# Conditional expert code: arms left out for the lower ranks, and the whole-array arm moved behind the others in one lane

## The chip, the cores and the metric

The kernel runs on one core of one Trainium2 chip, in one launch. The metric is device time in microseconds. Before the change the median of 3 runs is 1930.11 us (1925.82 to 1934.0). All rows below come from one profiled execution of 1932.14 us, whose span from the first to the last instruction is 1930.4 us.

The engines are TensorE (PE: matmuls and transposes; PEld is its weight loads), VectorE (DVE), ScalarE (ACT), GpSimd (POOL) and SyncE (SP, which issues the DMAs). Each engine has a sequencer of its own that runs its part of the program; a "q" behind the name (PEq) means the sequencer, which executes branches, register loads and semaphore instructions.

## The reference

Two trunk layers run over 256 latent and 256 context tokens of width 1024. Layer 0 mixes tokens with a gated position MLP and has a dense SwiGLU; layer 1 mixes with a bidirectional gated recurrence, and its channel mixer is a mixture of eight SwiGLU experts, of which each token uses two. Only that mixture is touched here. In the reference every expert runs over all tokens, and the weight of an unchosen expert is zero:

```python
logits = (hf @ w_router).astype(jnp.float32)
top_val, top_idx = lax.top_k(logits, TOP_K)            # TOP_K = 2, 8 experts
probs = jax.nn.softmax(top_val, axis=-1)
combine = jnp.sum(jax.nn.one_hot(top_idx, N_EXPERTS) * probs[..., None], axis=1)
for e in range(N_EXPERTS):                             # 1024 -> 3584 -> 1024 each
    out = out + combine[:, e:e + 1] * swiglu(hf, w_gate[e], w_up[e], w_down[e])
```

So 512 token places are shared among eight experts, and no expert has more than 256. How many each one gets is known only at run time.

## The kernel before

From about 868 us on the kernel runs the mixture; what comes earlier is the same in both versions. After the router, DVE counts the tokens of each expert and sorts: rank 0 is always expert 0, ranks 1 to 7 are the other experts by falling count. A table `Q` (12 rows of 8 numbers: positions, weights, counts) is permuted into the order of the ranks by one large multiply with a permutation mask and one reduce (L1354, L1356), giving `Qr`, whose integer copy `cnti` the sequencers load into registers: `rv`, the rows of an expert that its base unit takes (up to 128), and `ro`, the rows that go over into a second, "over" unit (L1229, L1230). SP loads seven base addresses of weights from it as well (L1360). A count of 65 to 96 is split into 64 base rows and the rest as over rows; otherwise only what exceeds 128 goes over.

Weights stream from memory in pieces of 1 MB (L222). The 3584 hidden columns are cut into seven chunks of 512. A whole region (kind "R") is one chunk of one expert: six pieces, gate and up matmuls (both at L1250), the down matmuls (L1277) of the chunk one or two regions earlier, transposes of its hidden block ahead of these (L1268), ACT's silu and DVE's product (L1283). Kind "F" has only the down part; "O" and "G" gather the next expert's rows (L1207, L1212), "S" scatters results (L1289).

Two lanes of regions are merged into one list by a fixed rule (`moe_regions`). The full lane holds ranks 1, 2, 3, the other lane ranks 0, 7, 6, 5, 4. Their regions alternate in stretches: rank 7 runs beside rank 1, rank 6 beside rank 2, rank 5 beside the end of 2 and the start of 3, rank 4 beside rank 3. The list is unrolled: each region is code of its own on every engine.

Inside a region the code has arms, chosen by `region()`. The base unit has three: n = 1, the whole 128x128 array, for more than 64 rows (`If` at L1317); n = 2, tiles of 64 rows with two parts of the contraction side by side, for 33 to 64 (`If` at L1320); and n = 4, tiles of 32 rows, for 32 or fewer. Then, where `ro > 0` (L1324), the over unit has two: n = 1 for more than 32 rows (L1325), else n = 4. For n = 2 and n = 4 the parts are added up by ACT and DVE (L1256 to L1260). One DVE, one ACT and one PE sequencer take each branch for themselves. An arm that is not taken is code that is jumped over. An over gather (L1235) and an over scatter (L1417) stand behind `If ro > 0` too.

In the order of a program a row "MATMUL ... x8" is eight matmuls, each of which the trace shows as two PE rows and two PEld rows. The four transposes of L1268 are two instructions each. So an arm of a whole region, with 24 matmuls and 4 transposes, is 104 instructions of PE.

With this data the trace shows these arms: rank 1 takes n = 1 and over n = 4; rank 2 takes n = 1 without over; rank 3 takes n = 2 and over n = 4; ranks 4 and 5 take n = 2; ranks 0, 6 and 7 take n = 4. Ranks 0, 2 and 4 to 7 have no over rows.

Of the kernel before, what the change touches and what calls it, by code (L numbers as in the profile page):

```python
# [9 lines left out]
F32 = mybir.dt.float32  # L10
F32R = mybir.dt.float32r
BF16 = mybir.dt.bfloat16
I32 = mybir.dt.int32
AF = mybir.ActivationFunctionType
ALU = mybir.AluOpType
AX = mybir.AxisListType

P = 128
# [4 lines left out]
NE = 8  # L23
# [245 lines left out]
def block_kernel(ctx, tc, xin, pos, cst, rows, wsT, adaS, adaT, wA, lruG, wr, wM, out):  # L269
    nc = tc.nc  # L270
    ACT, DVE, PE = nc.scalar, nc.vector, nc.tensor
# [37 lines left out]
    v = [va[:, 0], va[:, 1], vb[:, 0], vb[:, 1]]  # L309
# [724 lines left out]
    mp = ctx.enter_context(pool("mp", 1, "right"))  # L1034
    R = ExitStack()
    rp = R.enter_context(pool("rp", 1, "right"))
# [112 lines left out]
    pb = bank()  # L1149
# [2 lines left out]
    PE.matmul(pb[:, 8:16], tri, sb[:, 1], start=False, stop=True)  # L1152
    PE.matmul(pb[:, 16:24], onb, sb[:, 0], start=True, stop=False)
    PE.matmul(pb[:, 16:24], onb, sb[:, 1], start=False, stop=True)
    Q = mp.tile([P, 12, NE], F32, name="Q")
    posm, comb, few, m64, cb_, co_, e42 = Q[:, 0:2], Q[:, 2:4], Q[:, 4:8], Q[:, 8], Q[:, 9], Q[:, 10], Q[:, 11]
    DVE.scalar_tensor_tensor(posm, pb[:, 0:16].rearrange("p (t e) -> p t e", t=2), 1.0, sb, op0=ALU.add, op1=ALU.mult)
    cf = pb[:, 16:24]
    DVE.tensor_scalar(m64, cf, 64.0, 64.0, op0=ALU.is_gt, op1=ALU.mult)
    DVE.scalar_tensor_tensor(m64, cf, 96.0, m64, op0=ALU.is_le, op1=ALU.mult)  # L1160
    DVE.tensor_scalar(co_, cf, -128.0, None, op0=ALU.add)
    DVE.tensor_add(co_, co_, m64)
    DVE.tensor_scalar(co_, co_, 0.0, None, op0=ALU.max)
    DVE.tensor_sub(cb_, cf, co_)
    for n, (v, lim, m) in enumerate(((cb_, 64, 64), (cb_, 32, 32), (co_, 32, 64), (co_, 32, 32))):
        DVE.tensor_scalar(few[:, n], v, float(lim), -float(m), op0=ALU.is_le, op1=ALU.mult)
    dup = mp.tile([P, 2, P], F32, name="dup")
    DVE.memset(dup, 0.0)
    DVE.memset(dup[:, 0, 64:128], 1.0)
# [17 lines left out]
    class Expert:  # L1187
        def __init__(self, r, tab):
            self.e, self.s, self.n = r, LAG[r] - 1, (1, 2, 3).index(r) if r in (1, 2, 3) else (0, 7, 6, 5, 4).index(r)
            self.posm, self.comb, self.few, self.m64 = tab[:, 0:2], tab[:, 2:4], tab[:, 4:8], tab[:, 8, r:r + 1]  # L1190
            self.hh = hs_[self.s]

    def weigh(E, G, GT, ps, b):
# [25 lines left out]
    def gather_parts(E):  # L1219
        G = m2.tile([P, 2, P], F32, tag=f"G{E.s}", bufs=1, name="G")  # L1220
        sl_ = m2.tile([P, P], F32, tag="sl", bufs=1, name="sl")
        x = m2.tile([P, 8, P], F32, tag=f"x{E.s}", bufs=1, name="x")
        GT = m2.tile([P, 256], F32, tag=f"GT{E.s}", name="GT")
        ps = m2.tile([P, 1], F32, tag=f"ps{E.s}", name="ps")
        E.base = Unit(x, None, tg[:, E.s], GT, ps)

        def last():
            weigh(E, G, GT, ps, nb[0]())
            E.rv = nc.values_load(cnti[0:1, 0, E.e:E.e + 1], engines=ENG, min_val=0, max_val=128)  # L1229
            E.ro = nc.values_load(cnti[0:1, 1, E.e:E.e + 1], engines=ENG, min_val=0, max_val=128)  # L1230
        return [lambda: onehot(E, G, sl_, 0), lambda: gather(x, G, 0, nb[0]()), lambda: gather(x, G, 4, nb[0]()), last]

    def gather_over(E):
        U = E.over
        with tc.If(E.ro > 0):  # L1235
            onehot(E, Gu, slu, 1)
            gather(U.x, Gu, 0, bks[2 * par[0]])
            gather(U.x, Gu, 4, bks[2 * par[0] + 1])
            weigh(E, Gu, U.GT, U.ps, bks[2 * par[0]])

# [44 lines left out]
    def scatter(GT, src):  # L1285
        for hf in range(2):
            for t in range(2):
                b = nb[0]()
                PE.matmul(b, GT[:, t * P:(t + 1) * P], src[:, hf * 512:(hf + 1) * 512], start=True, stop=True)  # L1289
                a = acc[:, t, hf * 512:(hf + 1) * 512]  # L1290
                DVE.tensor_add(a, a, b)  # L1291
# [21 lines left out]
    def region(E, c, raws):  # L1313
        p0, p1 = bks[2 * par[0]:2 * par[0] + 2]
        lag = LAG[E.e]
        a = (p1, p0, p1, E.base.y, raws, c == lag, c == NCH + lag - 1, *hsel(E, c, E.hh))
        with tc.If(E.rv > 64) as c1:  # L1317
            chunk(E.base, 1, *a)
        with c1.Else():
            with tc.If(E.rv > 32) as c2:  # L1320
                chunk(E.base, 2, *a)
            with c2.Else():
                chunk(E.base, 4, *a)
        with tc.If(E.ro > 0):  # L1324
            with tc.If(E.ro > 32) as c3:  # L1325
                over(E, c, 1, raws)
            with c3.Else():
                over(E, c, 4, raws)
# [3 lines left out]
    E = exps[0]  # L1332
# [11 lines left out]
    DVE.tensor_scalar(ke[:, 0, 0:1], ke[:, 0, 0:1], 1024.0, None, op0=ALU.add)  # L1344
    DVE.tensor_scalar(ke[:, 1], slot[:, 0:NE], -1.0, None, op0=ALU.add)
    DVE.tensor_scalar(e42, ke[:, 1], float(6 * NCH), None, op0=ALU.mult)
    big = rp.tile([P, 12, NE, NE], F32, name="big")
    sq = lambda a: a[:, None, :].to_broadcast([P, NE, NE])
    tr = lambda a: a[:, :, None].to_broadcast([P, NE, NE])
    DVE.tensor_tensor(out=big[:, 0], in0=sq(ke[:, 0]), in1=tr(ke[:, 0]), op=ALU.is_gt)  # L1350
    DVE.tensor_reduce(ke[:, 0], big[:, 0], axis=AX.X, op=ALU.add)
    pm = rp.tile([P, NE, NE], F32, name="pm")
    DVE.tensor_tensor(out=pm, in0=sq(ke[:, 0]), in1=tr(ke[:, 1]), op=ALU.is_equal)
    DVE.tensor_tensor(out=big, in0=Q[:, :, None, :].to_broadcast([P, 12, NE, NE]), in1=pm[:, None].to_broadcast([P, 12, NE, NE]), op=ALU.mult)  # L1354
    Qr = mp.tile([P, 12, NE], F32, name="Qr")
    DVE.tensor_reduce(Qr, big, axis=AX.X, op=ALU.add)  # L1356
    cnti = mp.tile([P, 3, NE], I32, name="cnti")
    DVE.tensor_copy(cnti, Qr[:, 9:12])
    for r in range(1, NE):
        base42[r] = nc.values_load(cnti[0:1, 2, r:r + 1], engines=[mybir.EngineType.SP], min_val=0, max_val=6 * NCH * (NE - 1))  # L1360
    fs[3]()
    R.close()
    raw3 = ctx.enter_context(pool("raw3", 1, "right"))
# [40 lines left out]
    for kind, e, c in regs:  # L1404
        if kind == "O":
            exps[e] = Expert(e, Qr)
            parts[e] = gather_parts(exps[e])
            parts[e][0]()
        elif kind == "G":
            for f in parts[e][1:]:  # L1410
                f()
            start(exps[e])
        elif kind == "S":
            E = exps[e]
            nb[0] = yrot(E)
            scatter(E.base.GT, Ys[E.s])
            with tc.If(E.ro > 0):  # L1417
                DVE.tensor_scalar(E.over.y, E.over.y, E.over.ps, None, op0=ALU.mult)  # L1418
                scatter(E.over.GT, E.over.y)
            nb[0] = rot  # L1420
        else:
            E = exps[e]
            par[0] ^= 1
            rg = st.take_raw(2) if c < NCH else None
            rd = st.take_raw(2) if c >= LAG[e] else None
            ru = st.take_raw(2) if c < NCH else None
            region(E, c, (rg, rd, ru))
            for r in (rg, rd, ru):
                if r:
                    st.free(r)  # L1430
            if kind == "F" and c == NCH + LAG[e] - 1:
                ACT.activation(Ys[E.s][:, 0:512], E.base.y[0], AF.Copy, scale=E.base.ps)
                DVE.tensor_scalar(Ys[E.s][:, 512:1024], E.base.y[1], E.base.ps, None, op0=ALU.mult)
# [38 lines left out]
```

## Time and profile before

| what | value |
|---|---|
| median of 3 runs | 1930.11 us (1925.82 to 1934.0) |
| the profiled execution | 1932.14 us, span 1930.4 us |
| PE busy, of the span | 1698.4 us, 88% |
| DVE, ACT busy | 833.1 us (43%), 572.5 us (30%) |
| mean granted TensorE clock | 0.954 |
| DMA moved after 868 us | 343.18 MB, mean 323 GB/s |
| instruction packets (queue q8), before and after 868 us | 32 and 124 |

The mixture takes the span from about 868 us to the end, 1062 us, with PE busy most of it. Its idle time comes in short gaps between arms. The profile names for each gap who released the work: another engine's value, PE's own sequencer (PEq), or "issue", where nothing that it shows was waited for. Queue q8 carries instructions, q14 is small and also of the sequencers, and q1 carries data.

### The profile page before, as it was taken

The numbers are of one execution on the slowest core, as the hardware profiler recorded it, in microseconds if no ns is written. First come the engines' busy times: TensorE is split into PE (matmuls) and PEld (weight loads), VectorE is DVE, ScalarE is ACT, GpSimd is POOL, SyncE is SP. The second block draws the span as 40 slices with busy tenths as digits, with TensorE's granted clock in tenths as the row PEclk, the third lists the DMA queues.
The fourth block names the chain that finished last, engine by engine and source line by source line (L and its number), as shares of the span: only waits on it lengthen the run. The fifth ranks groups of instructions, "written<-read, shape, count | busy, mean of one in ns | idle before, by whom it ended". The sixth has DMA issues, their size and how long they took to land. (4 is left out here: it accounts for less than half of the span.)

```text
span 1930.4 us, 22052 instructions
## 1 busy us (share of the span) xinstructions
PE 1698.4 (88%) x8189; PEld 1038.2 (54%) x8189; DVE 833.1 (43%) x1326; ACT 572.5 (30%) x837; POOL 19.4 (1%) x22
## 2 busy tenths in 40 slices
PE   5999999998996999985888888889788998788886
PEld 2888888987885887773334333343334343323332
DVE  3777746576845448984211222131111122122133
ACT  5523226631212237971211122111111012121121
POOL 0000001000000000010000000000000000000000
PEclk9999999999997999997988999899989999999999
DMA  8654424356775513375885788877998979888980
GB/s 346 222 165 159 153 88 148 128 180 194 244 173 215 131 66 110 109 291 201 366 345 227 298 359 365 337 288 314 400 406 352 384 302 376 352 351 359 360 342 23
DMA packets 78669, 493.54 MB, mean 256 GB/s; under 512 B 16240, under 2 KB 16368, under 8 KB 20080
## 3 DMA queue, kind: packets, MB, share of 16 engines
q1 hardware_dynamic: 78448, 490.45, 66.8%
q8 instruction: 156, 2.56, 0.5%
q14 instruction: 65, 0.53, 0.1%
HBM read 489.34 MB, written 1.08 MB: 254 GB/s over the span
## 5 line engine op out<-in xcount | busy, mean ns | idle before, releaser
L1250 PE MATMUL ps<-raw,x 128*64 128x512 f32 (+2 forms) x1792 | 459.2, 644 | 28.6 <-issue 17.9
L1250 PEld LDWEIGHTS ps<-raw,x 128*64 128x64 f32 (+2 forms) x1792 | 167.9, 147 | 270.2 <-issue 255.7
L1277 PE MATMUL ps<-raw,hx 128*32 128x512 f32 (+2 forms) x1120 | 258.1, 628 | 13.5 <-ACT hx L1269 9.0
L520 PE MATMUL ps<-hThi,wh 128*128 128x512 f32 (+1 forms) x736 | 253.9, 346 | 3.0 <-ACT hThi L373 3.0
L521 PE MATMUL ps<-hTlo,wh 128*128 128x512 f32 (+1 forms) x736 | 252.1, 343 | 1.4 <-DVE hTlo L374 1.3
L522 PE MATMUL ps<-hThi,wl 128*128 128x512 f32 (+1 forms) x736 | 252.5, 344 | 0.0
L1257 DVE TENSOR_TENSOR ta__6611<-ps,ta__6611 64x512 f32<-64x512 f32 x112 | 76.5, 683 | 388.4 <-ACT ta__6611 L1256 332.0
L388 DVE SCALAR_TENSOR_TENSOR dj<-raw,srow 128x1024 bf16<-128x1024 f32 x128 | 156.2, 1220 | 92.6 <-DMA raw<-in_adaT_dram 89.1
L249 ACT CAST wh<-raw 128x2048 fp32r<-128x2048 f32 x69 | 131.4, 1909 | 205.2 <-PE ps L506 103.7
L250 DVE TENSOR_TENSOR wl<-raw,wh 128x2048 fp32r<-128x2048 f32 x69 | 158.8, 2304 | 58.0 <-ACT wh L249 57.6
L1277 PEld LDWEIGHTS ps<-raw,hx 128*32 128x32 f32 (+2 forms) x1120 | 93.3, 140 | 157.5 <-issue 128.1
L1256 ACT COPY ta__6611<-ps 64x512 f32<-64x512 f32 x112 | 65.2, 582 | 321.0 <-PE ps L1250 272.6
L520 PEld LDWEIGHTS ps<-hThi,wh 128*128 128x128 f32 x736 | 137.9, 188 | 21.4 <-ACT hThi L373 3.7
L521 PEld LDWEIGHTS ps<-hTlo,wh 128*128 128x128 f32 x736 | 138.2, 188 | 20.9 <-DVE hTlo L374 2.0
L522 PEld LDWEIGHTS ps<-hThi,wl 128*128 128x128 f32 x736 | 138.1, 188 | 18.0 <-issue 0.5
L504 PE MATMUL ps<-wh,ph 128*128 128x512 f32 x304 | 122.4, 403 | 16.9 <-ACT ph L609 16.9
L506 PE MATMUL ps<-wh,pl 128*128 128x512 f32 x304 | 121.4, 400 | 6.6 <-DVE pl L610 5.8
L1283 DVE TENSOR_TENSOR hx<-hx,ps 128x512 f32<-128x512 f32 x14 | 9.6, 688 | 261.7 <-PE ps L1250 186.7
L505 PE MATMUL ps<-wl,ph 128*128 128x512 f32 x304 | 120.8, 397 | 0.0
L1269 ACT COPY hx<-ps 128x128 f32<-128x128 f32 (+2 forms) x70 | 25.3, 361 | 247.0 <-PE ps L1268 240.1
L1250 PE MATMUL ps<-raw,xu 128*32 128x512 f32 x448 | 70.6, 642 | 22.8 <-DVE accy L1305 11.2
L504 PEld LDWEIGHTS ps<-wh,ph 128*128 128x128 f32 x304 | 58.3, 192 | 30.4 <-ACT ph L609 17.8
(319 smaller groups left out, 1665.5 us busy)
## 6 DMA issues: line engine op xcount, KB each, us to landing
raw<-in_wM_dram SPq DMA_DIRECT2D x336, 1024.0 KB, 11.7
raw<-in_wA_dram SPq DMA_DIRECT2D x69, 1024.0 KB, 4.9
raw<-in_adaT_dram SPq DMA_DIRECT2D x40, 1024.0 KB, 5.3
va<-in_adaS_dram SPq DMA_DIRECT2D x4, 1024.0 KB, 10.6
ysum<-in_xin_dram SPq DMA_DIRECT2D x4, 512.0 KB, 5.2
vb<-in_adaS_dram SPq DMA_DIRECT2D x2, 1024.0 KB, 9.8
srow<-in_adaS_dram SPq DMA_DIRECT2D x2, 1024.0 KB, 11.5
lw<-in_lruG_dram SPq DMA_DIRECT2D x8, 256.0 KB, 3.1
```

Source lines behind the costliest of these rows:

```text
L249: self.nc.scalar.copy(wh, raw)
L250: self.nc.vector.tensor_tensor(out=wl, in0=raw, in1=wh.bitcast(F32), op=ALU.subtract)
L388: DVE.scalar_tensor_tensor(j, raw[:, kk * D:(kk + 1) * D], 1.0, srow[:, vv], op0=ALU.mult, op1=ALU.mult, accum_out=adaC[l, bb // 8][:, bb ...
L504: PE.matmul(o, lh, rh, start=start, stop=False)
L505: PE.matmul(o, lh, rl, start=False, stop=False)
L506: PE.matmul(o, ll, rh, start=False, stop=stop)
L520: PE.matmul(o, wh[:, r], hThi[:, kk, c0:c1], start=(kk == 0), stop=False)
L521: PE.matmul(o, wh[:, r], hTlo[:, kk, c0:c1], start=False, stop=False)
L522: PE.matmul(o, wl[:, r], hThi[:, kk, c0:c1], start=False, stop=(kk == 7))
L1250: PE.matmul(o[m * g:m * g + m], x[:, kb, 0:m], raws[kb // 4][1][:, (kb % 4) * 512:(kb % 4 + 1) * 512], start=(r == 0), stop=(r == 8 // n - ...
L1257: DVE.tensor_tensor(out=ta_[0:64], in0=o[0:64], in1=ta_[0:64], op=ALU.add)
L1277: PE.matmul(yb_[hf][m * g:m * g + m], U.th[:, kk * m:(kk + 1) * m], rd[hf][1][:, kk * 512:(kk + 1) * 512], start=(first and r == 0), stop= ...
```

## The change

- Ranks 4 to 7 lose the over unit: no over gather, no over part of a region (`If` at L1324 with its two arms), no over scatter, and no register `ro`. For these ranks a count of 65 to 96 is no longer split; they keep the three base arms.
- Rank 1 loses its n = 4 arm.
- In the full lane (ranks 1, 2, 3) the test is turned round: a new register `rl` is 1 where the base rows are 64 or fewer. `If rl > 0` comes first with the n = 2 and n = 4 arms, and the n = 1 arm stands last, behind `Else`. Rank 0 and ranks 4 to 7 keep the old order.
- The table has 13 rows; the permuting multiply and reduce cover the first six, and the derived rows (`units`) are computed again from the permuted counts, by small DVE operations. The base addresses for SP are cast before that.

```diff
-    Q = mp.tile([P, 12, NE], F32, name="Q")
+    Q, Qr = [mp.tile([P, 13, NE], F32, name=f"Q{n}") for n in range(2)]
...
+    def units(q):
+        few, m64, cb_, co_ = q[:, 6:10], q[:, 10], q[:, 11], q[:, 12]
...
+        if q is Qr:
+            DVE.memset(m64[:, 4:NE], 0.0)
...
-            E.ro = nc.values_load(cnti[0:1, 1, E.e:E.e + 1], engines=ENG, min_val=0, max_val=128)
+            if E.e < 4:
+                E.ro = nc.values_load(cnti[0:1, 1, E.e:E.e + 1], engines=ENG, min_val=0, max_val=128)
+            if E.e in (1, 2, 3):
+                E.rl = nc.values_load(cnti[0:1, 3, E.e:E.e + 1], engines=ENG, min_val=0, max_val=1)
...
     def gather_over(E):
         U = E.over
+        if E.e >= 4:
+            return
...
-        with tc.If(E.rv > 64) as c1:
-            chunk(E.base, 1, *a)
-        with c1.Else():
+
+        def few_():
+            if E.e == 1:
+                return chunk(E.base, 2, *a)
             with tc.If(E.rv > 32) as c2:
                 chunk(E.base, 2, *a)
             with c2.Else():
                 chunk(E.base, 4, *a)
+
+        if E.e in (1, 2, 3):
+            with tc.If(E.rl > 0) as c1:
+                few_()
+            with c1.Else():
+                chunk(E.base, 1, *a)
+        else:
+            with tc.If(E.rv > 64) as c1:
+                chunk(E.base, 1, *a)
+            with c1.Else():
+                few_()
+        if E.e >= 4:
+            return
         with tc.If(E.ro > 0):
...
-    DVE.tensor_tensor(out=big, in0=Q[:, :, None, :].to_broadcast([P, 12, NE, NE]), in1=pm[:, None].to_broadcast([P, 12, NE, NE]), op=ALU.mult)
-    Qr = mp.tile([P, 12, NE], F32, name="Qr")
-    DVE.tensor_reduce(Qr, big, axis=AX.X, op=ALU.add)
-    cnti = mp.tile([P, 3, NE], I32, name="cnti")
-    DVE.tensor_copy(cnti, Qr[:, 9:12])
+    DVE.tensor_tensor(out=big, in0=Q[:, 0:6, None, :].to_broadcast([P, 6, NE, NE]), in1=pm[:, None].to_broadcast([P, 6, NE, NE]), op=ALU.mult)
+    DVE.tensor_reduce(Qr[:, 0:6], big, axis=AX.X, op=ALU.add)
+    cnti = mp.tile([P, 4, NE], I32, name="cnti")
+    DVE.tensor_copy(cnti[:, 2], Qr[:, 5])
     for r in range(1, NE):
         base42[r] = nc.values_load(cnti[0:1, 2, r:r + 1], engines=[mybir.EngineType.SP], min_val=0, max_val=6 * NCH * (NE - 1))
+    units(Qr)
+    DVE.tensor_copy(cnti[:, 0:2], Qr[:, 11:13])
+    DVE.tensor_scalar(cnti[:, 3], Qr[:, 6], 0.0, None, op0=ALU.is_lt)
...
-            with tc.If(E.ro > 0):
-                DVE.tensor_scalar(E.over.y, E.over.y, E.over.ps, None, op0=ALU.mult)
-                scatter(E.over.GT, E.over.y)
+            if e < 4:
+                with tc.If(E.ro > 0):
+                    DVE.tensor_scalar(E.over.y, E.over.y, E.over.ps, None, op0=ALU.mult)
+                    scatter(E.over.GT, E.over.y)
```

Over the whole program PE's order falls from 12127 matmuls to 10267; the branch and matmul rows printed for it fall from 5620 to 5118. Line numbers move: L1317 becomes L1345 (rank 0 and the other lane) or L1340 (full lane), L1320 becomes L1334, L1324 becomes L1351, L1250 becomes L1263, L1268 becomes L1281, L1277 becomes L1290.

PE before, at the end of a region of rank 6 and up to the code of rank 2's next one (the last arm of rank 6's base, and its over part with the first of its two arms):

```order
L1250 MATMUL ps<-raw,x 32x512 x8
L1320 UNCONDITIONAL_BRANCH
L1324 COMPARE_AND_BRANCH
L1325 COMPARE_AND_BRANCH
L1268 MATMUL ps<-ident,hu_6616 128x128 x4
L1250 MATMUL ps<-raw,xu_6613 128x512 x8
L1277 MATMUL ps<-raw,hx 128x512 x8
L1250 MATMUL ps<-raw,xu_6613 128x512 x8
L1325 UNCONDITIONAL_BRANCH
L1268 MATMUL ps<-ident,hu_6616 128x32 x4
```

PE after, at the same place (the same last arm of rank 6's base, then rank 2's region):

```order
L1263 MATMUL ps<-raw,x 32x512 x8
L1334 UNCONDITIONAL_BRANCH
L1340 COMPARE_AND_BRANCH
L1334 COMPARE_AND_BRANCH
L1281 MATMUL ps<-ident,hx 128x64 x4
L1263 MATMUL ps<-raw,x 64x512 x8
L1290 MATMUL ps<-raw,hx 64x512 x8
L1263 MATMUL ps<-raw,x 64x512 x8
L1334 UNCONDITIONAL_BRANCH
L1281 MATMUL ps<-ident,hx 128x32 x4
```

Before, two over arms stand between rank 6's work and rank 2's, and rank 2's n = 1 arm comes first. After, rank 2's n = 2 and n = 4 arms stand there in their place, and its n = 1 arm comes behind them.

DVE before, at the sorting of the table:

```order
L1353 TENSOR_TENSOR pm<-ke 128x64
L1354 TENSOR_TENSOR big<-Q,pm 128x768
L1356 TENSOR_REDUCE Qr<-big 128x96
L1215 COPY x<-ps 128x512
L1358 CAST cnti<-Qr 128x24
L1199 COPY ps<-ps 128x1
```

DVE after, at the same place (`Q_6405` is the table, `Q_6406` the permuted one):

```order
L1381 TENSOR_TENSOR big<-Q_6405,pm 128x384
L1382 TENSOR_REDUCE Q_6406<-big 128x48
L1384 CAST cnti<-Q_6406 128x8
L1163 TENSOR_SCALAR Q_6406<-Q_6406 128x8
L1167 TENSOR_SCALAR Q_6406<-Q_6406 128x8
L1164 SCALAR_TENSOR_TENSOR Q_6406<-Q_6406 128x8
L1166 MEMSET Q_6406 128x4
L1168 TENSOR_TENSOR Q_6406<-Q_6406 128x8
```

The two large operations halve, the addresses for SP are cast right behind them, and nine to ten small operations on the permuted table follow before the two remaining casts.

## Rows read from the trace of the kernel before

**Rows 1.** The page, part 1: busy time, share, instructions.

```profile
PE 1698.4 (88%) x8189; PEld 1038.2 (54%) x8189; DVE 833.1 (43%) x1326; ACT 572.5 (30%) x837; POOL 19.4 (1%) x22
```

**Rows 2.** Waits of PE, 880 to 1925: line, waited for, us, times, longest.

```profile
engine line waited for: us in total, times, longest us
PE ps L1268 <- PEq L1324: 18.2, 15, 4.2
PE ps L1250 <- issue: 17.9, 3, 14.0
PE ps L1268 <- issue: 16.6, 4, 5.7
...
PE ps L1250 <- DMA raw<-in_wM_dram: 0.8, 1, 0.8
```

**Rows 3.** Timeline of PE, 1343 to 1410.

```profile
start us, us, engine line op out<-in xcount [idle before <-releaser]
...
1352.97 1.92 PE L1250 MATMUL ps<-raw,x 128*32 128x512 f32 x16
1354.71 1.94 PE L1277 MATMUL ps<-raw,hx 128*32 128x512 f32 x16
1356.43 1.94 PE L1250 MATMUL ps<-raw,x 128*32 128x512 f32 x16
1364.06 0.63 PE L1268 MATMUL ps<-ident,hb 32*128 32x32 f32 x4 [5.69 <-issue]
1364.62 3.64 PE L1250 MATMUL ps<-raw,x 128*32 128x512 f32 x16
1368.03 3.17 PE L1277 MATMUL ps<-raw,hx 128*32 128x512 f32 x16
1371.03 1.90 PE L1250 MATMUL ps<-raw,x 128*32 128x512 f32 x16
1373.28 0.65 PE L1268 MATMUL ps<-ident,hx 128*128 128x128 f32 x4 [0.35 <-PEq L1324]
```

**Rows 4.** Branches and semaphores of line 1324 on PE's queue.

```profile
engine op xcount: duration ns min/median/max, first and last start us, forms
L1324 PEldq COMPARE_BRANCH  x69: 70/337/6332, 896.8 to 1903.2; - x69
L1324 PEldq EVENT_SEMAPHORE  x53: 51/51/51, 897.1 to 1907.7; - x53
```

**Rows 5.** The branch at line 1320, 1358 to 1366.

```profile
L1320 PEldq COMPARE_BRANCH  x1: 5162/5162/5162, 1358.8 to 1358.8; - x1
```

**Rows 6.** DMA queues, 0 to 868: packets, MB, share.

```profile
q8 instruction: 32, 0.52, 0.2%
```

**Rows 7.** DMA queues, 868 to the end.

```profile
DMA packets 47477, 343.18 MB, mean 323 GB/s; under 512 B 5264, under 2 KB 5264, under 8 KB 5904
...
q8 instruction: 124, 2.03, 0.8%
```

**Rows 8.** DMA queues, 1358 to 1374.

```profile
DMA packets 923, 6.72 MB, mean 420 GB/s; under 512 B 106, under 2 KB 106, under 8 KB 106
...
q8 instruction: 3, 0.05, 1.2%
```

**Rows 9.** Windows by stage: the first layers, and ranks 6 and 2.

```profile
core 0: us, PE busy (x) PEld busy (x) DVE busy (x) ACT busy (x) POOL busy (x), PEclk, DMA share, GB/s
0.00:868.00 868.00, 812.92 (x4066) 665.07 (x4067) 575.17 (x882) 377.01 (x475) 13.30 (x18) 0.98 0.52 173
...
1297.00:1484.00 187.00, 158.03 (x651) 65.72 (x650) 33.30 (x52) 29.47 (x54) 0.00 (x0) 0.94 0.90 365
```

**Rows 10.** Windows, short ones: the granted clock.

```profile
1352.00:1358.40 6.40, 5.75 (x52) 2.02 (x52) 1.93 (x3) 2.06 (x4) 0.00 (x0) 1.00 0.90 328
...
1364.00:1371.00 7.00, 6.94 (x36) 2.03 (x40) 1.36 (x2) 1.43 (x3) 0.00 (x0) 0.53 1.02 422
```

**Rows 11.** Timeline of PE: the first and the last long gap.

```profile
1123.57 0.60 PE L1268 MATMUL ps<-ident,hb 32*128 32x32 f32 x4 [4.19 <-ACT ta__6611 L1256]
...
1821.42 0.68 PE L1268 MATMUL ps<-ident,hx 64*128 64x64 f32 x4 [2.83 <-PEq L1324]
```

**Rows 12.** Timeline of PE, 928 to 1015.

```profile
967.51 0.43 PE L1268 MATMUL ps<-ident,hb 32*128 32x32 f32 x4 [4.16 <-PEq L1324]
...
978.95 1.11 PE L1268 MATMUL ps<-ident,hx 128*128 128x128 f32 x4 [3.33 <-PEq L1324]
```

**Rows 13.** Groups of PE by shape, 880 to 1925.

```profile
L1250 PE MATMUL ps<-raw,x 128*128 128x512 f32 x448 | 202.5, 607 | 0.9 <-ACT ps L1259 0.5 <-PEq L1324 0.5
```

**Rows 14.** Timeline of DVE, 866 to 884.

```profile
876.70 0.96 DVE L1354 TENSOR_TENSOR big<-Q,pm 128x768 f32<-128x768 f32 x1
877.70 0.95 DVE L1356 TENSOR_REDUCE Qr<-big 128x96 f32<-128x768 f32 x1
```

More of the change, by code (lines that the diff above doesn't have):

```diff
@@ L1154, in block_kernel @@
     PE.matmul(pb[:, 16:24], onb, sb[:, 1], start=False, stop=True)
-    Q = mp.tile([P, 12, NE], F32, name="Q")
-    posm, comb, few, m64, cb_, co_, e42 = Q[:, 0:2], Q[:, 2:4], Q[:, 4:8], Q[:, 8], Q[:, 9], Q[:, 10], Q[:, 11]
+    Q, Qr = [mp.tile([P, 13, NE], F32, name=f"Q{n}") for n in range(2)]
+    posm, comb, cf, e42 = Q[:, 0:2], Q[:, 2:4], Q[:, 4], Q[:, 5]
     DVE.scalar_tensor_tensor(posm, pb[:, 0:16].rearrange("p (t e) -> p t e", t=2), 1.0, sb, op0=ALU.add, op1=ALU.mult)
[L1158 to L1166, printed above, removed]
+    DVE.tensor_copy(cf, pb[:, 16:24])
+    def units(q):
+        few, m64, cb_, co_ = q[:, 6:10], q[:, 10], q[:, 11], q[:, 12]
+        cf = q[:, 4]
+        DVE.tensor_scalar(m64, cf, 64.0, 64.0, op0=ALU.is_gt, op1=ALU.mult)
+        DVE.scalar_tensor_tensor(m64, cf, 96.0, m64, op0=ALU.is_le, op1=ALU.mult)
+        if q is Qr:
+            DVE.memset(m64[:, 4:NE], 0.0)
+        DVE.tensor_scalar(co_, cf, -128.0, None, op0=ALU.add)
+        DVE.tensor_add(co_, co_, m64)
+        DVE.tensor_scalar(co_, co_, 0.0, None, op0=ALU.max)
+        DVE.tensor_sub(cb_, cf, co_)
+        for n, (v, lim, m) in enumerate(((cb_, 64, 64), (cb_, 32, 32), (co_, 32, 64), (co_, 32, 32))):
+            DVE.tensor_scalar(few[:, n], v, float(lim), -float(m), op0=ALU.is_le, op1=ALU.mult)
+    units(Q)
     dup = mp.tile([P, 2, P], F32, name="dup")
@@ L1189, in __init__ @@
             self.e, self.s, self.n = r, LAG[r] - 1, (1, 2, 3).index(r) if r in (1, 2, 3) else (0, 7, 6, 5, 4).index(r)
-            self.posm, self.comb, self.few, self.m64 = tab[:, 0:2], tab[:, 2:4], tab[:, 4:8], tab[:, 8, r:r + 1]
+            self.posm, self.comb, self.few, self.m64 = tab[:, 0:2], tab[:, 2:4], tab[:, 6:10], tab[:, 10, r:r + 1]
             self.hh = hs_[self.s]
@@ L1346, in block_kernel @@
     DVE.tensor_scalar(e42, ke[:, 1], float(6 * NCH), None, op0=ALU.mult)
-    big = rp.tile([P, 12, NE, NE], F32, name="big")
+    big = rp.tile([P, 6, NE, NE], F32, name="big")
     sq = lambda a: a[:, None, :].to_broadcast([P, NE, NE])
```

## The prediction

> **What bounds the kernel now.** I read the page's busy times first. PE is busy for 88% of the span, DVE for 43%, ACT for 30% [rows 1], so the end is set by PE's work and by what keeps PE idle. The matmuls that run are the same after the change: the arms taken with this data stay the same. Only PE's idle time, and the clock behind it, can move.
>
> The waits of PE come next. Data is no reason for them: matmuls waited for a weight transfer once, 0.8 us [rows 2]. But L1268, the transposes that open an arm, waited 18.2 us for PE's own sequencer and 16.6 us for "issue", and L1250 another 17.9, of which one wait of 14.0 is the start of the mixture [rows 2]. These are waits at branches.
>
> What the sequencer does there is seen at 1358. A region of rank 6 ends with the row at 1356.43; the next one, also n = 4, starts at 1364.06 after 5.69 us idle [rows 3]. In it lies one branch at L1320 that took 5.16 us [rows 5], where a branch takes 0.07 us at its shortest [rows 4], and in these 16 us the instruction queue q8 carried 3 packets [rows 8]. So the sequencer waits for code.
>
> How much code is fetched: before 868 us 4066 + 4067 PE instructions [rows 9] came with 32 packets [rows 6], 254 to a packet. After it PE executes 8189 x 2 [rows 1] less these, some 8,250, yet 124 packets move [rows 7], room for 31,500. The arms that are jumped over are fetched as well, in order. An arm of 104 instructions is 0.41 packet; rank 6's jump from the end of one n = 4 arm to the next one (two over arms, n = 1, n = 2) is 1.6 packets, in which PE has only 5.8 us of matmuls (1.92 + 1.94 + 1.94 [rows 3]) to hide them.
>
> A second cost sits at the same place. Where L1324 is false, PE's sequencer executes a semaphore instruction, 53 times [rows 4], and it waits there until PE's matmuls are through. It is seen even where no code is late: 0.35 us before rank 2's arm [rows 3].
>
> A third is the clock. [...]
>
> **The change, part by part.** The sum goes against the profiled execution, 1932.1 us (span 1930.4); this is 2.0 above the median, so 2 comes off at the end.
>
> *(a) The over units of ranks 4 to 7 go.* By tile shape (32 and 64 rows) I went through PE's timeline. Twelve gaps of 2 us or more stand ahead of arms of these ranks, the first 4.19, the last 2.83 us [rows 11], 39.7 us together. With them go shorter ones, 21 of 0.3 to 1.1 us like the 0.35 in [rows 3], 9 together: 48.5 us. By the branch that was slow in each gap, 34.5 of it is fetching and 14 is the semaphore at L1324 (36 of its 53 executions are of these ranks). The 14 goes with the branch itself: the instruction is no longer there. Of the fetch part I don't take all: rank 6's jump shrinks from 4 arms to 2, that is from 1.6 packets to 0.8, and some jumps still cross into a packet that is late behind a short arm. I leave two such waits of 3 us, 6 in all (bounds 0, and 17, half of it, as if each remaining half jump kept its share). Gain 42.5.
>
> *(b) The clock behind these gaps.* By the same comparison as at 1364 the arms behind the twelve gaps lost 20.7 us, from 0 to 2.9 each. It comes back with the gaps: I take it in proportion to the net gaps, (a) less (c): 36.5 of 48.5, so 15.6 (bounds 5 and 20.7).
>
> *(c) The n = 1 arm behind the others in the full lane.* Ranks 1 and 2 run n = 1 in 14 regions (448 rows of 128*128 by 32 a region [rows 13]). Their jump moves from the end of a long arm, whose 7.03 us groups hide a fetch, to its start, behind a short arm of the other lane. At rank 2 the number of arms skipped ahead of it stays at two: over arms of rank 6 before, n = 2 and n = 4 of rank 2 now; there the wait was 0.35 us [rows 3]. At rank 1 the other lane's neighbour is rank 0 first, which keeps its over arms: there two waits of 4.16 and 3.33 us are there now and stay [rows 12], and the entry becomes three arms long instead of two. I take 4 more us there (bounds 0 and 9). Rank 3 takes n = 2, and now jumps over n = 4 and n = 1 behind it: 2 us (0 to 5). Loss 6.
>
> *(d) The sorting.* Two DVE operations of 0.96 and 0.95 us [rows 14] halve, which saves about 0.8; a copy and nine to ten operations of some 0.2 us come, and part of them lies behind the cast that SP waits for. Against that SP gets its addresses some 2 us sooner. PE stands idle here for 14.0 us, of which its register loads are most, and one load of 16 goes. I take 0 (bounds 1 lost, 2.6 gained).
>
> *(e) What is late next: transfers.* In the stretch of ranks 6 and 2, 187 us, data moves at 365 GB/s [rows 9], and 420 is what a full stretch reaches [rows 8]. 187 x 365 / 420 is 162.5, so no more than 24.5 us can go there. Of (a) and (b) some 27 us fall into this stretch. I take 3 off (0 to 6). ACT and DVE wait for PE at their branches, never the other way by these gaps; their shorter code costs nothing.
>
> Sum: 42.5 + 15.6 - 6 - 3 = 49. 1932.1 - 49 = 1883, against the median **1881 us**.
>
> [...] The trace shows 124 packets for some 8,250 executed instructions [rows 7, 9], so what is skipped is paid for. [...]
>
> **The rivals.**
>
> *R1, a jump costs its fetch whatever its length.* Then waits at the jumps over n = 1 and n = 2 stay, and what goes is what stands at the removed branches alone: by the slow branches 8.5 us at L1324, 4.9 at the over gathers and scatters and their neighbours, and the 14 of the semaphores: 27.4. 1932.1 - 27.4 - 2 = 1903. For it: the longest branch, 6.33 us, is at L1324 [rows 4]. Against it: the packet count above, which follows the length of the code. [...]
>
> *R2, only the semaphore goes.* The fetch waits come from something that is not the length of the code, and move to the branches that remain. 14 us: 1932.1 - 14 - 2 = 1916. For it: the short gaps at L1324 are many and regular. Against it: the three packets inside the 16 us of 1358 [rows 8]. [...]
>
> *R3, slower: the entries of the full lane.* The 14 n = 1 regions are each entered behind a jump over two arms, when only a short arm of the other lane lies between. An exposed entry costs what a long gap costs now: 39.7 / 12 = 3.3 us, with 20.7 / 12 = 1.7 us of clock, 5.0 together; 14 of them are 70. The gain of (a) and (b) without (c) is at most 57, so it is slower from 12 exposed entries on: 70 - 57 = 13, 1943. For it: the entries behind rank 0 wait already, 3.33 us [rows 12]. Against it: at rank 2, where the skipped length is unchanged, the wait now is 0.35.
>
> *R4, more.* All of the fetch goes, nothing of (c) comes, the transfers keep up: 48.5 + 20.7 + 2.6 = 72, 1858; below that only with shifts of packet bounds that I don't see.
>
> **How the numbers follow.** The forecast with its bounds ((a) and (c) both bad give about 24 of gaps, some 8 of clock: 1898; both good, 1860): chance 0.60, own range 1860 to 1897. R1 0.17, R2 0.08, R3 0.06, R4 0.05, no effect at all 0.04. Faster by over 0.5% (9.65 us, about what a measurement of this kernel can tell from no change) is below 1920.5: 0.60 + 0.17 + 0.05 and most of R2, 0.07, so 0.89. Same 0.06, slower 0.05. For 8 in 10 the range takes in R1 and R4: 1852 to 1907.
>
> **What would show it.** Instruction packets after 868 us fall from 124 to about 95 (12127 - 10267 = 1860 matmuls less, at four instructions some 7,400, 29 packets). The semaphore at what was L1324 is executed 17 times, not 53. L1281 waits for "issue" and PEq for under 15 us together instead of 34.8. In the loop of ranks 6 and 2 the clock is above 0.97 and the DMA above 400 GB/s. R1 would show the waits of 3 to 6 us at L1345 and L1334 of ranks 6 and 7; R3 at L1340, ahead of tiles of 128 rows. I am wrong if packets fall as said and the waits don't, or if gaps go and PE then waits for raw weights or for DVE's and ACT's sums instead.

## The result, and the profile after

The changed kernel takes 1881.48 us at the median (1879.17 to 1882.59, 4 runs), the kernel before on the same chip 1928.21 us (1925.82 to 1934.0, 4 runs): a ratio of 0.9752, 95% interval 0.9726 to 0.9777. The forecast was 1881. The profiled execution after took 1881.16 us, its span 1879.2 us against 1930.4.

Part 1 of the page, busy time, share and instructions:

```profile
PE 1685.1 (90%) x8189; PEld 1034.8 (55%) x8189; DVE 832.9 (44%) x1340; ACT 572.3 (30%) x837; POOL 19.4 (1%) x22
```

The instructions of PE are as many as before [rows 1]; they were busy 13.3 us less, and the rest of the 51.2 us is idle time that went.

The waits of PE in the mixture (line, what was waited for; us in total, times, longest):

```profile
PE ps L1263 <- PEq L1351: 11.9, 2, 10.8
PE ps L1263 <- issue: 11.6, 4, 4.6
...
PE ps L1281 <- DVE ta__6625 L1273: 7.1, 2, 3.8
PE ps L1281 <- issue: 6.0, 5, 1.7
...
PE ps L1263 <- DMA raw<-in_wM_dram: 3.5, 3, 1.4
...
PE ps L1281 <- PEq L1351: 1.4, 2, 0.7
PE ps L1290 <- DMA raw<-in_wM_dram: 1.4, 2, 0.9
```

What L1268 waited for PE's own branches and "issue", 34.8 us [rows 2], is 7.4 at L1281. Two waits beside rank 0 have only changed their name: the 4.16 and 3.33 us of [rows 12] are 3.79 and 3.33 now, put to DVE (first L1281 row), though behind branches of PE of 3.26 and 3.04 us as before; counted alike, 34.8 became 14.5. All waits at this line together fell from 64.5 to 29.8 us. In their place waits for weights appear, 4.9 us against 0.8: PE has come nearer to its transfers. Of the 11.9 at L1263, 10.8 is the start of the mixture.

The branches and the semaphore of the line that was L1324 (times in ns, min/median/max), and the DMA of the mixture with the instruction queue:

```profile
L1351 PEldq COMPARE_BRANCH  x33: 65/202/3260, 898.4 to 1845.7; - x33
L1351 PEldq EVENT_SEMAPHORE  x17: 51/51/51, 898.8 to 1554.8; - x17
```

```profile
DMA packets 47577, 343.63 MB, mean 340 GB/s; under 512 B 5280, under 2 KB 5280, under 8 KB 5920
...
q8 instruction: 96, 1.57, 0.6%
```

The semaphore is executed 17 times instead of 53 [rows 4], and 96 packets of code move instead of 124 [rows 7].

The timeline of PE at the place of [rows 3], two regions of rank 6 and the start of one of rank 2 (start, length, work, idle time before):

```profile
1340.51 1.94 PE L1263 MATMUL ps<-raw,x 128*32 128x512 f32 x16
1342.75 0.43 PE L1281 MATMUL ps<-ident,hb 32*128 32x32 f32 x4 [0.31 <-issue]
1343.11 1.92 PE L1263 MATMUL ps<-raw,x 128*32 128x512 f32 x16
1344.85 1.94 PE L1290 MATMUL ps<-raw,hx 128*32 128x512 f32 x16
1346.57 2.64 PE L1263 MATMUL ps<-raw,x 128*32 128x512 f32 x16
1349.14 0.66 PE L1281 MATMUL ps<-ident,hx 128*128 128x128 f32 x4
...
1377.98 0.66 PE L1281 MATMUL ps<-ident,hx 128*128 128x128 f32 x4 [0.99 <-issue]
```

The gap of 5.69 us is 0.31, and the n = 4 matmuls behind it take 1.92 + 1.94 + 2.64 us instead of 3.64 + 3.17 + 1.90: the clock didn't fall, it is 1.00 under all three. Some waits stay: 0.99 ahead of a later region of rank 2, with "issue" as its reason, behind a branch at L1340 of 3.3 us.

The windows of the loop of ranks 6 and 2, and of ranks 4 and 3:

```profile
core 0: us, PE busy (x) PEld busy (x) DVE busy (x) ACT busy (x) POOL busy (x), PEclk, DMA share, GB/s
...
1284.20:1459.30 175.10, 154.28 (x653) 63.73 (x653) 33.32 (x52) 29.47 (x54) 0.00 (x0) 0.97 0.92 375
...
1691.40:1855.20 163.80, 150.22 (x788) 56.32 (x788) 43.92 (x65) 36.10 (x68) 0.00 (x0) 0.99 0.83 341
```

The first of these was 187.0 us at a clock of 0.94 [rows 9] and is 175.1 at 0.97.

PE executes the same matmuls in the same order in both kernels, so both traces can be cut at the same matmul and the parts compared. This table is worked out from the rows of all PE matmuls in the two traces, in us; its first stretch begins at the first matmul, at 13.5 and 14.0 us:

```
stretch (cut at the same matmuls)   before  after   less idle  less busy
up to 937 us                         923.6   923.1     1.7       -1.2
rank 0 beside rank 1                  78.4    77.5     0.3        0.6
rank 7 beside rank 1                 282.2   269.6     8.3        4.3
rank 6 beside rank 2                 187.1   175.1     8.3        3.7
rank 5 beside rank 2                 113.9   111.9     4.0       -2.1
rank 5 beside rank 3                 123.7   120.2     3.0        0.6
rank 4 beside rank 3                 181.8   163.9    11.2        6.8
the end                               16.4    14.1     1.8        0.5
```

From rank 7 on, 36.5 us of idle time are gone, and 13.8 us of busy time with them. A second trace of the changed kernel, `after_again` below, agrees with the first within 0.5 us of idle time there; its busy time is 3.2 us longer, so busy time of one trace is not surer than that.

### The profile page after: what moved, and what is told of

Its sections match the earlier page's. It is cut to its first block, busy times and chain, and to the rows that moved or that the text cites. A ratio compares the mean times of both kernels' runs of the same rounds, so it can differ in the third digit from the quotient of the medians.

```text
span 1879.2 us, 21723 instructions
## 1 busy us (share of the span) xinstructions
PE 1685.1 (90%) x8189; PEld 1034.8 (55%) x8189; DVE 832.9 (44%) x1340; ACT 572.3 (30%) x837; POOL 19.4 (1%) x22
## 5 line engine op out<-in xcount | busy, mean ns | idle before, releaser
L1263 PE MATMUL ps<-raw,x 128*64 128x512 f32 (+2 forms) x1792 | 441.7, 613 | 28.3 <-PEq L1351 11.9
L1263 PEld LDWEIGHTS ps<-raw,x 128*64 128x64 f32 (+2 forms) x1792 | 162.8, 143 | 261.5 <-issue 244.7
L1290 PE MATMUL ps<-raw,hx 128*32 128x512 f32 (+2 forms) x1120 | 259.2, 626 | 18.2 <-ACT hx L1282 15.1
L249 ACT CAST wh<-raw 128x2048 fp32r<-128x2048 f32 x69 | 131.4, 1908 | 203.7 <-PE ps L506 95.5
L1290 PEld LDWEIGHTS ps<-raw,hx 128*32 128x32 f32 (+2 forms) x1120 | 92.3, 138 | 161.9 <-issue 123.1
L522 PEld LDWEIGHTS ps<-hThi,wl 128*128 128x128 f32 x736 | 138.9, 189 | 17.5 <-issue 0.5
L1263 PE MATMUL ps<-raw,xu 128*32 128x512 f32 x448 | 69.5, 633 | 21.6 <-DVE accy L1318 11.4
## 6 DMA issues: line engine op xcount, KB each, us to landing
raw<-in_wM_dram SPq DMA_DIRECT2D x336, 1024.0 KB, 13.7
va<-in_adaS_dram SPq DMA_DIRECT2D x4, 1024.0 KB, 10.6
vb<-in_adaS_dram SPq DMA_DIRECT2D x2, 1024.0 KB, 10.8
srow<-in_adaS_dram SPq DMA_DIRECT2D x2, 1024.0 KB, 12.2
```

The source lines that it names most:

```text
L249: self.nc.scalar.copy(wh, raw)
L522: PE.matmul(o, wl[:, r], hThi[:, kk, c0:c1], start=False, stop=(kk == 7))
L1263: PE.matmul(o[m * g:m * g + m], x[:, kb, 0:m], raws[kb // 4][1][:, (kb % 4) * 512:(kb % 4 + 1) * 512], start=(r == 0), stop=(r == 8 // n - ...
L1290: PE.matmul(yb_[hf][m * g:m * g + m], U.th[:, kk * m:(kk + 1) * m], rd[hf][1][:, kk * 512:(kk + 1) * 512], start=(first and r == 0), stop= ...
```

## The experiments

Two theories are set against each other. L: code that is jumped over is fetched in order, so its length is paid for wherever PE's queue doesn't cover it. J: a jump has its price whatever its length. A third, S, was that the semaphore alone counted. The kernels were measured in groups; those of a group share a chip and the runs of the kernel before, which took 1923.5, 1923.0 and 1919.8 us there. The expectations in us were made from the first measurement, so across groups it is the ratios that are compared. In the traces of the changed kernel and its variants the stretch up to 937 us, nearly the same code in all of them, lasts 912.6 to 925.4 us, and 914.8 to 922.7 on one chip. So traces are compared by the stretches behind it, cut at the same matmuls as above.

| kernel | median us | ratio to before, 95% interval | packets after 868 us |
|---|---|---|---|
| dead_arms | 1932.57 | 1.0052 (1.0032 to 1.0072) | 119 |
| tiny_if | 1886.67 | 0.9802 (0.9768 to 0.9837) | 96 |
| over_only | 1872.22 | 0.9742 (0.9705 to 0.9779) | 98 |
| order_only | 1964.62 | 1.0201 (1.0160 to 1.0243) | 121 |
| after_again | 1874.46 | 0.9744 (0.9717 to 0.9770) | 96 |
| best | 1863.42 | 0.9693 (0.9665 to 0.9721) | 95 |
| over_only_5 | 1871.54 | 0.9731 (0.9703 to 0.9759) | 98 |
| long_arm | 1941.59 | 1.0115 (1.0074 to 1.0155) | 118 |
| half_arm | 1887.96 | 0.9824 (0.9785 to 0.9862) | 107 |
| shift | 1874.96 | 0.9760 (0.9719 to 0.9801) | 96 |
| two_arms | 1860.18 | 0.9679 (0.9641 to 0.9717) | 90 |

**Does the length of code that never runs cost time?** First with dead arms between the n = 2 and the n = 4 arm:

```diff
             with c2.Else():
-                chunk(E.base, 4, *a)
+                if E.e >= 4:
+                    with tc.If(E.rv > 64) as c4:
+                        chunk(E.base, 1, *a)
+                        chunk(E.base, 4, *a)
+                    with c4.Else():
+                        chunk(E.base, 4, *a)
+                else:
+                    chunk(E.base, 4, *a)
```

> The changed kernel, with two whole arms of dead code (n = 1 and n = 4) put back into every region of ranks 4 to 7, between the n = 2 and the n = 4 arm, behind a test that is never true there; nothing of it is executed, and no If without an Else is added, so the semaphore of the removed If does not come back. Theory L (the length of skipped code is paid for): the fetch part of the gain comes back and the semaphore part stays gone. Of the 36 us of gaps that the change took away at ranks 4 to 7, some 22 return, and about 8 of clock: near 1912 us (1900 to 1922), instruction packets back to about 120. Rival J (a jump costs its fetch, whatever its length): the jumps are as many as in the changed kernel, so 1881 (within 5). Rival S (only the semaphore counted): 1881 (within 5).

It lost more than the whole gain: 1932.57 us, 1.0052 of the kernel before. Its new branch (times in ns) waited 4.3 us at the median:

```profile
L1338 PEldq COMPARE_BRANCH  x18: 208/4339/5882, 1051.1 to 1527.8; - x18
```

L was right in sign and too low in size. J wasn't ruled out, since a region with n = 4 executes one more test and jump than in the changed kernel; my expectation had called the jumps as many. So the dead code was put inside the n = 1 arm, where no branch is added:

```diff
             with tc.If(E.rv > 64) as c1:
                 chunk(E.base, 1, *a)
+                if E.e >= 4:
+                    chunk(E.base, 1, *a)
+                    chunk(E.base, 4, *a)
             with c1.Else():
                 few_()
```

> The changed kernel with two whole arms of dead code inside the n = 1 arm of ranks 4 to 7, which no expert takes with this data. The same jumps are executed as in the changed kernel, not one more, and no semaphore; only the jump over the n = 1 arm is three arms long instead of one. (In the kernel with dead arms run before, an n = 4 region executed one test and one jump more, so that run does not tell length from the number of jumps.) Theory L: the time of the kernel with dead arms, 45 to 55 us over the changed kernel, packets near 120. Rival J: no difference from the changed kernel, within 4 us; packets near 96. Halfway (the added jump of the other run cost part of it): 20 to 30 us.

67 us slower than the changed kernel beside it, where L expected 45 to 55. The branches of PE at the n = 1 test and behind it (ns), in the changed kernel and then in this one, the second also on DVE and ACT; the timeline of PE in the loop of ranks 6 and 2, and the instruction queue:

```profile
L1345 PEldq COMPARE_BRANCH  x45: 202/218/4030, 884.4 to 1850.3; - x45
L1334 PEldq COMPARE_BRANCH  x79: 65/179/2395, 884.7 to 1854.0; - x79
```

```profile
L1345 PEldq COMPARE_BRANCH  x45: 202/342/6906, 877.1 to 1907.2; - x45
L1334 PEldq COMPARE_BRANCH  x79: 65/212/5877, 877.4 to 1910.9; - x79
L1334 DVEq COMPARE_BRANCH  x79: 43/50/56, 877.4 to 1909.5; - x79
L1334 ACTq COMPARE_BRANCH  x79: 34/40/45, 877.1 to 1910.4; - x79
```

```profile
1375.77 0.51 PE L1281 MATMUL ps<-ident,hb 32*128 32x32 f32 x4 [4.31 <-DVE hx L1296]
...
1410.11 0.60 PE L1281 MATMUL ps<-ident,hx 32*128 32x32 f32 x4 [5.78 <-issue]
...
1444.28 0.60 PE L1281 MATMUL ps<-ident,hb 32*128 32x32 f32 x4 [5.68 <-issue]
...
1455.86 0.60 PE L1281 MATMUL ps<-ident,hx 32*128 32x32 f32 x4 [4.29 <-DVE hb L1296]
```

```profile
q8 instruction: 118, 1.93, 0.7%
```

45 and 79 branches as in the changed kernel, yet four of the short arms of rank 6 in a row start 4.3 to 5.8 us late. Ahead of each of the four, a branch of PE at L1334 took 4.8 to 5.9 us and ended 0.2 us before the arm. Two of the rows name DVE, but the arm doesn't need that value: in the changed kernel the same transposes start at 1342.75, while DVE ends the product of the region before at 1345.88. That code is late on DVE or ACT, which jump over the dead arms too, is ruled out by their branches: 0.06 us at most. J falls: the number of jumps is the same, the length is not. Half the dose leaves out the first of the two added arms:

```diff
                 chunk(E.base, 1, *a)
+                if E.e >= 4:
+                    chunk(E.base, 4, *a)
```

> The changed kernel with one whole arm of dead code, not two, inside the n = 1 arm of ranks 4 to 7. Theory L, with a cover: PE's queue hides the first part of a jump and not the last, so half of the code costs less than half of what two arms cost (that was some 65 us at the medians, 54 in the two profiles): 15 to 30 us over the changed kernel, packets near 107. If each packet has its price wherever it is: 27 to 35.

```profile
q8 instruction: 107, 1.75, 0.7%
```

1887.96 us, a ratio 0.008 over the changed kernel's, or 15 us. By the ratios eleven packets cost about 15 us and the next eleven about 56 (0.9824 to 1.0115). By the traces, against `after_again` and from rank 7 on, it is 21 and 40 us, of these 17.7 and 29.3 idle: the second half costs more by both, how much more is not settled. The idle time says where:

```
idle us added, by stretch           first arm   second arm
ranks 7 and 6 (run n = 4)             14.5        15.7
ranks 5 and 4 (run n = 2)              3.3        13.7
```

Behind the short arms of n = 4 (5.8 us of matmuls a region) each added arm costs the same, from the first on. Behind the arms of n = 2, with three groups of 3.65 us or 11 us a region (1754.06 to 1764.63 in the trace of the changed kernel), the first added arm is nearly free and the second is not. So a packet has no fixed price: by this reading PE's matmuls cover a jump as long as they last, and what is longer is paid.

**What is the semaphore worth?**

```diff
         if E.e >= 4:
+            with tc.If(E.rv > 127):
+                m = 32
+                PE.transpose(p1[:, 0:m], a[8][0:m, 0:P], ident[0:m, 0:m])
+                ACT.copy(E.base.th[:, 0:m], p1[:, 0:m])
             return
```

> The changed kernel, with a last If put back into every region of ranks 4 to 7 that is never true and holds one transpose and one ACT copy: the branch and the semaphore on its false path are back (36 more on PE), the code is not. Theory L: only the semaphore part returns, 14 us of gaps, with some more since the sequencer no longer runs ahead over what it still has to fetch, and 3 to 6 of clock: 1897 (1890 to 1907), packets about 97. Rival J: the fetches at these jumps return as well, 27 us of gaps and 10 of clock: 1918. Rival S: all of the gain is lost: 1928.

The 36 semaphores are back (second row, ns), and 12.1 us of waits at L1281 with them (third row, from the waits):

```profile
L1350 PEldq COMPARE_BRANCH  x36: 202/208/458, 1061.4 to 1861.5; - x36
L1350 PEldq EVENT_SEMAPHORE  x36: 51/51/51, 1064.9 to 1866.0; - x36
```

```profile
PE ps L1281 <- PEq L1350: 12.1, 20, 0.9
```

By the ratios it is 11 us slower than the changed kernel (0.9802 to 0.9744), by the traces from 937 us on 14.6 us against the first one of the changed kernel and 11.9 against the second. L wanted 16 (9 to 26) over the changed kernel. Each of the 36 semaphores begins 0.04 to 0.12 us behind the end of the last matmul, up to 6.9 us after its own branch was through: it waits until PE has run dry. The branches took 0.46 us at most, so an If that holds next to no code costs this wait and no fetch. J and S, which wanted 37 and 47 us over the changed kernel, fall.

**Which half of the change brings it?** The first kernel, `over_only`, takes the full lane's order back, and with it rank 1's n = 4 arm; its edit is shown. The second, `order_only`, is the kernel before with the full lane's new order and without rank 1's n = 4 arm:

```diff
-        if E.e in (1, 2, 3):
-            with tc.If(E.rl > 0) as c1:
-                few_()
-            with c1.Else():
-                chunk(E.base, 1, *a)
-        else:
-            with tc.If(E.rv > 64) as c1:
-                chunk(E.base, 1, *a)
-            with c1.Else():
-                few_()
+        with tc.If(E.rv > 64) as c1:
+            chunk(E.base, 1, *a)
+        with c1.Else():
+            few_()
```

> The changed kernel with the full lane in its old order: n = 1 first for ranks 1 to 3, and rank 1 keeps its n = 4 arm; the over units of ranks 4 to 7 stay away. Theory L: the same code but for 7 arms, only placed elsewhere: what is spared at the entry of the full lane is paid at its exit; within 6 us of the changed kernel, 1876 to 1888. Rival E (the entries of the full lane cost, 5 us each where exposed): 1860 to 1875, as those entries are gone. A third reading, that the whole gain is from the order of the arms: 1920 to 1930.

> The kernel before with the full lane alone changed: n = 1 last for ranks 1 to 3, rank 1 without n = 4; all over units stay. Theory L: seven arms less of 280 and the same semaphores: 1922 to 1934, no clear difference from before. Rival E: 5 us for each exposed entry, up to 70: 1935 or more. A third reading, that the order brings the gain: below 1910.

The removal alone gives the whole gain: 1872.22 us, a ratio of 0.9742 against 0.9752 and 0.9744 of the changed kernel. (As a time it lies in the range that E wanted; by the ratio, 1878 us of the first measurement, it doesn't.) The order alone costs 41 us, 2%; the traces put 28 us of idle time in it from rank 7 on, 16.9 of them in the loop of ranks 6 and 2. I had expected no difference from L there, and that was a slip in applying it: with the over arms still in place, the entry to rank 2's n = 1 arm lies behind four arms instead of two, and what stands before it is a short arm of rank 6. The timeline of PE shows it (tiles of 128 rows are rank 2's entries, of 32 rank 6's), and the branch that is now the first at the full lane's entry (ns):

```profile
1350.88 1.12 PE L1270 MATMUL ps<-ident,hx 128*128 128x128 f32 x4 [9.16 <-issue]
...
1386.74 0.63 PE L1270 MATMUL ps<-ident,hb 32*128 32x32 f32 x4 [6.02 <-issue]
...
1398.66 0.78 PE L1270 MATMUL ps<-ident,hx 128*128 128x128 f32 x4 [3.57 <-DVEq L1338]
```

```profile
L1329 PEldq COMPARE_BRANCH  x24: 70/338/6588, 932.7 to 1925.4; - x24
```

This is the mechanism of the slower rival, at the price that it has while the over arms are there.

**Undoing the order in the changed kernel.** Rank 1 without n = 4 in the old order, the changed kernel, and the kernel with the removal alone (`best`, `after_again`, `over_only_5`), on one chip:

```diff
# "best", against over_only
+            if E.e == 1:
+                return chunk(E.base, 2, *a)
             with tc.If(E.rv > 32) as c2:
                 chunk(E.base, 2, *a)
```

> The changed kernel as it is, to stand on the same chip as the runs sent with it. On the chip of the four runs before, the part of the program ahead of 868 us ran some 8 to 10 us shorter than in the first measurement, in kernels whose code there is the same, so only what runs together is compared. Expected ratio to the kernel before 0.973 to 0.978, by every theory.

> The changed kernel with the full lane in its old order (n = 1 first), and rank 1 without its n = 4 arm: all of the removed code stays removed, only the order is undone. Theory L, with what order_only showed (an arm placed ahead of the full lane's n = 1 arm is paid behind a short arm): the order costs 3 to 6 us once the over units are gone, so this is 3 to 7 us faster than the changed kernel. Rival J: the same jumps, the same time within 2 us. If the order of the changed kernel is what brings its gain: slower than it.

> The changed kernel with the full lane in its old order and rank 1 with its n = 4 arm, once more and beside the changed kernel itself. Theory L: 2 to 5 us faster than the changed kernel, and 0 to 3 slower than the version without rank 1's n = 4 arm. Rival J: equal to the changed kernel.

1863.42, 1874.46 and 1871.54 us: the old order with all the removed code gone is 11 us faster than the changed kernel. Removal with rank 1's n = 4 arm kept is 3 us faster than the changed kernel at the medians, which the intervals don't separate. Not all of the 11 is shown to be the order's. By the traces cut at the same matmuls, 5.9 us lie where rank 1 is entered beside rank 0 (3.1 idle, 2.7 busy). The timelines of PE there, of the changed kernel and then of the old order:

```profile
967.34 0.63 PE L1281 MATMUL ps<-ident,hb 32*128 32x32 f32 x4 [3.79 <-DVE ta__6625 L1273]
...
979.21 0.66 PE L1281 MATMUL ps<-ident,hx 128*128 128x128 f32 x4 [3.33 <-DVE ta__6625 L1273]
```

```profile
963.94 0.43 PE L1281 MATMUL ps<-ident,hb 32*128 32x32 f32 x4 [3.74 <-DVE ta__6625 L1273]
...
971.70 0.65 PE L1281 MATMUL ps<-ident,hx 128*128 128x128 f32 x4 [0.35 <-PEq L1345]
```

The 3.33 us ahead of rank 1's arm [rows 12] are 0.35. But the kernel before has the old order too and waits 3.33 there; what may differ is where the packets begin. That was tried by itself, with half a packet of dead code at one place, ahead of everything:

```diff
                 chunk(E.base, 1, *a)
+                if (E.e, c) == (0, 0):
+                    chunk(E.base, 1, *a)
+                    chunk(E.base, 4, *a)
```

> The changed kernel with two arms of dead code at one place only, in the n = 1 arm of rank 0's first region (gate and up matmuls only, half a packet): from there on all code stands half a packet later. Theory L: the total is the same but for half a packet, yet which jumps cross into a late packet changes: within 6 us of the changed kernel either way, with waits at other places. If the waits hung on the jumps alone: the same waits at the same places.

```profile
970.94 0.49 PE L1281 MATMUL ps<-ident,hb 32*128 32x32 f32 x4 [3.00 <-DVE ta__6625 L1273]
...
978.82 0.66 PE L1281 MATMUL ps<-ident,hx 128*128 128x128 f32 x4 [0.47 <-PEq L1354]
```

The wait ahead of the 128-row tiles is 0.47 with the new order as well, and other gaps opened (2.84 us from 1199.69 on, 2.90 from 1409.23 on in its trace). No change of the time can be told: ratio 0.9760 against 0.9744. So a wait at one place is partly luck of the packet's edge, and the 5.9 us can't be put down to the order. Nor can the rest: from rank 7 on `best` has no less idle time than the changed kernel (0.0 us; 0.5 against the first trace), and its 5.6 us (2.4) less of busy time are hardly more than the 3.2 by which two traces of the changed kernel differ. What the order costs once the over arms are gone lies between nothing and 11 us.

**Is there more of it?**

```diff
+        if E.e >= 6:
+            few_()
+        else:
+            with tc.If(E.rv > 64) as c1:
+                chunk(E.base, 1, *a)
+            with c1.Else():
+                few_()
...
-                chunk(E.base, 2, *a)
+                chunk(E.base, 1 if E.e >= 6 else 2, *a)
```

> The version with the full lane in its old order and rank 1 without n = 4, with the n = 2 arm of ranks 6 and 7 taken out as well (their If at 64 rows goes; an expert of these ranks with 33 to 64 rows, which this data has not, is not computed rightly). Theory L: each jump at ranks 6 and 7 is one arm shorter; what is left there of waits for code is 7 to 10 us, so 4 to 10 us faster than that version, packets near 89. If what is left there is not waits for code: no difference.

1860.18 us at 0.9679 against 0.9693, with 90 packets: by the ratios no difference that can be told. In the traces its loop of ranks 6 and 2 is 6.3 us shorter, 4.5 of it idle time, within the 4 to 10 that L wanted. In this trace PE still waits 12.2 us for "issue" and its own branches, besides 10.7 at the start of the mixture; most of its other waits are put to other engines' values. So not much more is in sight by leaving out code.

## Why the prediction was right, point by point

- *The number*: 1881 forecast, 1881.48 measured. The mechanism holds, but the half microsecond is luck: the gain is 46.7 us by the medians and 51 between the two profiled executions, against 49 summed, and terms below are off by several us in both directions.
- *What bounds the kernel*: shown. With the same jumps, code that never runs moved the time by 15 and by 67 us.
- *(a) The over units*: forecast 48.5 us of gaps, 6 of which stay, and (c) took 6 of gaps more: 36.5 net, or 33.5 if the 3 of (e) are idle time too. The cut traces give 36.5. With the removal alone (`over_only`) they give 38.1, where (a) said 42.5, or 39.5 less (e). So (a) was 1 to 4 us too high, and the net is right because (c) took less than forecast. The places are not right: ranks 7 and 6 gave 8.3 each, where the long gaps promised about 11 and 20, since waits of code stay there (4.57 us ahead of rank 5's first region, where 2.81 was, 1.74 and 0.99 ahead of rank 2's arms). Two of the twelve gaps, 2.94 and 2.49 us, stand ahead of 128-row arms of ranks 1 and 2, behind over arms of ranks 7 and 6, not ahead of the lower ranks' own arms. The semaphore's 14 us was borne out by the kernel with the empty If: 11 by the ratios, 11.9 and 14.6 by the traces.
- *(b) The clock*: 15.6 forecast, 13.8 measured as busy time of the same matmuls, with the 3 us of doubt named above. The 20.7 us that it starts from are added up from groups like the three at 1364: 8.71 us [rows 3] at a clock of 0.53 from 1364 to 1371, against 5.80 at 1.00 ahead of the gap [rows 10], 2.9 lost.
- *(c) The order*: 6 forecast, not shown. At rank 1's entry nothing was lost against the kernel before (0.3 us gained). From rank 7 on the new order has 1.6 us more of idle time than `over_only` in one pair of traces and 0.4 less in the other. Undoing it gains 3 to 11 us by the kernel, 5.9 of the 11 at rank 1's entry, 3.1 of it idle time; a shift of half a packet alone took one wait there from 3.33 to 0.47 us. That the same edit costs 41 us while the over arms are there I didn't see ahead, nor in the expectation of that run; in the prediction it appears only as the slower rival, which put the exposed entries at 5 us each without asking how long the jump is.
- *(d) The sorting*: 0 forecast. The wait at the start of the mixture went from 14.0 to 10.8 us. Only 0.7 of it is ahead of the semaphore at L1324 (10.6 before, 9.9 after), where the sorting counts; the rest lies behind that branch, and 1.5 us come back at the next wait.
- *(e) The transfers*: 3 forecast; PE's waits for weights grew by 4.1. But the loop of ranks 6 and 2 reached 375 GB/s, not the 400 that I named as a sign, and went down by 12.0 us, far from the 24.5 that transfers allow by my estimate from 420 GB/s [rows 8]. PE waited there 8.3 us for "issue" and its own branches and 4.9 for weights.
- *Signs*: packets 96 (about 95 forecast), semaphores 17 (17), clock of the loop 0.97 (above 0.97). The waits of L1281 for "issue" and PEq are 7.4 (under 15), 14.5 with the two that are put to DVE now.
- *The range*: its bad end was added up wrongly. (a) at 31.5 and (c) at 14 leave 17.5 us of gaps, not 24, with 7.5 of clock and 3 off for transfers some 1908, not 1898. The result doesn't come near it.
- *Skipped code*: fetched too, by these runs: the two dead arms of `long_arm` brought 22 packets (96 to 118). With four arms of 104 instructions skipped ahead of an n = 4 arm of rank 6, a branch of PE took 5.16 us in the kernel before [rows 5] and 4.8 to 5.9 us in `long_arm`.

## What to carry to other kernels

Count instruction packets against executed instructions; where far more code is fetched than run, arms that arithmetic rules out for any data are worth removing, by the idle time behind short arms and the lower clock after it (here 36.5 us idle and 13.8 us of longer matmuls). Here, of 512 places the fourth of seven sorted counts can't exceed 128, and as expert 0 has at most 256, the largest of the seven can't be under 37. Place skipped code behind long work: by the dose runs a jump costs that part of its length that the matmuls queued ahead of it don't cover (the first added arm 14.5 us of idle time behind regions of 5.8 us, 3.3 behind those of 11). And judge an order of arms only together with the length of the code around it: the same edit cost 41 us with the over arms in place, and without them 3, which can't be told from none.

## What the runs showed of the hardware that wasn't expected

- The price of skipped code is not in proportion to its length: 11 packets cost 15 us by the ratios or 21 by the traces, 11 more 56 or 40. Behind the 5.8 us regions of ranks 7 and 6 both arms cost alike (14.5 and 15.7 us idle), behind the 11 us regions of ranks 5 and 4 only the second (3.3 and 13.7).
- Only TensorE's sequencer was late: the same branch took up to 5.9 us there and 0.06 us at most on VectorE and ScalarE.
- A shift of all code by half a packet moved single waits of 3 us to other places, without a change of the time that can be told, 0.9760 (0.9719 to 0.9801) against 0.9744 (0.9717 to 0.9770).
- An If without an Else that is never true cost 0.3 to 0.4 us each (11 to 14.6 us by 36), at branches of 0.21 us at the median: its semaphore begins 0.04 to 0.12 us behind the last matmul.
